# One sum of raw weights per pair of gate and up: VectorE addition or accumulating DMA

## The chip, the cores and the metric

The kernel runs on one core of a Trainium2 chip. The core has five engines that this text calls by their names in the profile: PE (TensorE, the matrix multiplier), PEld (its weight loads), DVE (VectorE), ACT (ScalarE), POOL (GpSimd) and SP (SyncE, which here only issues transfers). The metric is device time in microseconds (us); lower is better. All inputs are float32 in HBM, and the result has to match a float32 reference.

## What is computed

Two decoder layers over 512 tokens of width 1024. Each has a SwiGLU block, a mixing block (sliding-window attention beside a short convolution) and a second SwiGLU block; a norm stands before each and at the end.

```python
def swiglu(h, w_gate, w_up, w_down):          # 1024 -> 2816 -> 1024
    return (jax.nn.silu(h @ w_gate) * (h @ w_up)) @ w_down

def reference(x, ...):
    for l in range(2):
        x = x + 0.5 * swiglu(rms_norm(x, ffn1_norm[l]), ffn1_wg[l], ffn1_wu[l], ffn1_wd[l])
        h = rms_norm(x, mix_norm[l])
        z = h @ w_in[l]
        ...
        x = x + jnp.concatenate([attn_out, conv_out], axis=-1) @ w_out[l]
        x = x + 0.5 * swiglu(rms_norm(x, ffn2_norm[l]), ffn2_wg[l], ffn2_wu[l], ffn2_wd[l])
    return rms_norm(x, final_norm)
```

There are four SwiGLU blocks in all; the text numbers them 1 to 4 in their order.

## The kernel before

**Precision.** Every weight group of 128x1024 float32 values is split before it is used: ACT casts it to a rounded high part (`wh`, 1.04 us), and DVE subtracts that from the raw values to get the low part (`wl`, 1.22 us). Both are in `split`, line 228. PE then makes three products per tile: high by high, high by low, low by high. So each group costs one ACT cast and one DVE subtraction, and PE reads `wl` for the first time in the third matmul on the group (`stream`, line 831 on).

**Seven products instead of eight.** Gate and up are taken together as a matrix of two by two blocks: rows are the two halves of the 1024 inputs, columns are gate and up. Call the blocks a11 and a12 (gate, first and second half of the inputs) and a21 and a22 (up). One such stage of 512 gate and 512 up columns is a *pair* below; a block has `("w", b)` with b = 1, 3, 5, 7, 9. The pair is made with seven products of half the tokens instead of eight, and these take seven forms of the weights, in the order of `FORMS`: a11, a12, s2, s3, s1, a22, s4, where

- s1 = a21 + a22,
- s2 = a11 + s1,
- s3 = a11 + a21,
- s4 = a12 + s2.

Each form is held in two groups, h = 0 and 1, so a pair has 14 groups. PE works on one group for 2.72 us and on one form for 5.44 us. The down-projection of 8 blocks of 128 rows is done likewise, in stages `("s", 1)` and `("s", 5)`; the output projection of the mixing block too. The fourth SwiGLU block has `("s", 1)` and then an end of its own.

**Where the sums are made.** `seven` (line 375) lists the loads of a stage: ten units, a11, s1, a12, s3, a22, each for h = 0 and 1. A unit with two sources is loaded from its first source by SP and then the second source is added to it by an accumulating DMA from POOL (`need_raw`, lines 221 to 223). That is so for s1 (a21, then a22 added) and s3 (a21, then a11 read from HBM a second time and added). The other two sums are made in SBUF while the forms are split, in `need_split`: s2 by a DVE addition into a11 (line 269), and s4 by adding a11, which by then holds s2, into a12. In a pair of gate and up that last one is a DVE addition (line 291); in a stage whose `how` is "share", which is every stage of the down-projection and of the output projection, it is an accumulating DMA from SBUF to SBUF, issued by POOL (line 289).

**What sets the order.** `take_split` is called when PE's work on a group is written out; it asks for the split of the group two further on (`SPLIT_AHEAD` = 2), and for raw loads four or more units ahead of that. There are three buffers for `wh` and three for `wl`, so the split of group n+2 can begin when PE has finished group n-1. There are eight buffers for raw units, so a load waits until the last reader of the unit that held its buffer is done. The instructions are not put in order by hand here: a planner orders each engine's instructions when the kernel is built, by data dependences, by the order of the program text and by its own estimate of durations; `issue_after` puts an instruction behind another. On the chip every engine then works through its list in that fixed order. The loads go through SP's list and the accumulating DMAs through POOL's.

**The first pair of a block.** In the pair b = 1 the first group (a11, h = 0) is split with "far": the low part comes from an accumulating DMA, not from DVE. Around this pair DVE also evicts the first small down-projection (line 1268) and makes and splits the forms of the activations (lines 601 to 606 and 228). In the first block this is arranged differently (`near`).

Of the kernel before, what the change touches and what calls it, by code (L numbers as in the profile page):

```python
# [75 lines left out]
def trunk_kernel(  # L76
# [23 lines left out]
    nc = tc.nc  # L100
# [92 lines left out]
    units = []  # L193
# [6 lines left out]
    def add_unit(*unit):  # L200
        units.append(unit)
        return len(units) - 1
# [24 lines left out]
    def split(hi, lo, raw, eng=nc.vector):  # L227
        return nc.scalar.copy(hi, raw), eng.tensor_sub(lo, raw, f32(hi))  # L228

    def split_far(hi, lo, raw):  # L230

        nc.scalar.activation(lo, raw, AF.Copy, scale=-1.0)
        nc.scalar.copy(hi, raw)
        return nc.gpsimd.dma_start(out=f32(lo), in_=raw, accum_op=ALU.add)

    def need_split(g):
        while state["split"] <= min(g, len(order) - 1):
            n = state["split"]
            u, what = order[n]
            far = what == "far"  # L240
            if what in (None, "far"):
                need_raw(u if far else max(u, min(u + LOAD_AHEAD, state["hold"] or len(units))))
                raw = raw_of.pop(u)
            elif isinstance(what, tuple) and what[0] == "end":

                _, what, h = what
                at = {"a11": 2, "s2": 2, "s3": 3, "s1": 3, "a12": 4, "a22": 5, "s4": 5}[what]
                need_raw(u + 3 * at + h + LOAD_AHEAD)
                raws = {name: u + 3 * i + h for i, name in enumerate(END_LOADS)}
                if what == "s2":  # L250
                    with tc.issue_after(state["rest"]):
                        nc.vector.tensor_add(raw_of[raws["a11"]], raw_of[raws["a11"]], raw_of[raws["s1"]])
                raw = raw_of[raws["a11" if what in ("s2", "s4") else what]]
            elif isinstance(what, tuple):

                what, h, how = what
                far = how == "far"
                last = {"a11": 0, "a12": 4, "s2": 2, "s3": 6, "s1": 2, "a22": 8, "s4": 4}[what]
                need_raw(u + h if far else u + max(last, 4) + h + LOAD_AHEAD)
                a11, s1, a12, s3, a22 = (raw_of.get(u + 2 * i + h) for i in range(5))  # L260
                if what == "s2":

                    late = state["late"] if h else None
                    if not state["late"] and how == "share":
                        late = state["rest"]
                    if how == "behind":
                        late = state["mark"]
                    with tc.issue_after(late) if late else nullcontext():
                        nc.vector.tensor_add(a11, a11, s1)  # L269
                raw = {"a11": a11, "a12": a12, "s2": a11, "s3": s3, "s1": s1, "a22": a22, "s4": a12}[what]  # L270
            shape = list(raw.shape)
            hi = wpool.tile(shape, F32R, tag="wh", bufs=3, name=f"wh_{n}")
            lo = wpool.tile(shape, F32R, tag="wl", bufs=3, name=f"wl_{n}")
            if far:
                sent = split_far(hi, lo, raw)
            else:
                state["cast"], state["rest"] = (i.ins for i in split(hi, lo, raw))
                if isinstance(order[n][1], tuple) and order[n][1][2] == "mark":
                    state["mark"] = state["rest"]
            if isinstance(order[n][1], tuple) and order[n][1][0] == "end":  # L280
                if what == "a12":
                    nc.gpsimd.dma_start(out=raw_of[raws["a11"]], in_=raw, accum_op=ALU.add)
                if what in ("s3", "s1", "a12", "a22"):
                    del raw_of[raws[what]]
                if what == "s4":
                    del raw_of[raws["a11"]]
            elif isinstance(order[n][1], tuple):
                if what == "s3" and how == "share":
                    nc.gpsimd.dma_start(out=a12, in_=a11, accum_op=ALU.add)
                elif what == "s3":  # L290
                    nc.vector.tensor_add(a12, a12, a11)
                done = {"s3": (0, 3), "s1": (1,), "a22": (4,), "s4": (2,)}.get(what, ())
                for i in done:
                    del raw_of[u + 2 * i + h]
            split_of[n] = (hi, lo)
            state["split"] += 1
            if far:

                with tc.issue_after(sent.ins):
                    need_raw(u + LOAD_AHEAD + (4 + h if isinstance(order[n][1], tuple) else 0))  # L300
# [26 lines left out]
    def abreast(kc):  # L327

        return max(1, KC // kc) if kc in (2, 4) else 1
# [34 lines left out]
    def plan():  # L364
        def cols(src, k0, kc, n, how=None, last=False):
            wide = abreast(kc)
            for b in halves_of(n, wide, last):
                order.append((add_unit((src, k0, kc, b * P, wide * P)), how))

        def plain(wg, wu, b):  # L370
            for w in (wg, wu):
                for j in range(2):
                    order.append((add_unit((w, 0, KC, (2 * b + j) * P, P)), None))

        def seven(at, how):


            u = len(units)
            for what in (((0, 0),), ((1, 0), (1, 1)), ((0, 1),), ((1, 0), (0, 0)), ((1, 1),)):
                for h in range(2):  # L380
                    add_unit(*(at(o, j, h) for o, j in what))
            order.extend((u, (what, h, how(what, h))) for what in FORMS for h in range(2))

        def ffn(wg, wu, wd, stages, near=False):
            for what, b in stages:
                how = "far" if b == (0,) and not near else None
                if what == "p":
                    plain(wg, wu, b)
                if what == "w":
                    seven(  # L390
                        lambda o, j, h: ((wg, wu)[o], KC // 2 * j + 2 * h, 2, 2 * b * P, S),
                        lambda what, h: "far"
                        if (b, what, h) == (1, "a11", 0)
                        else {("a12", 0): "mark", ("s2", 1): "behind"}.get((what, h))
                        if near and b == 3
                        else None,
                    )
                if what == "s":
                    seven(
                        lambda o, j, h: (wd, 2 * b + KC // 2 * j + 2 * h, 2, o * S, S),  # L400
                        lambda what, h: "share",
                    )
                if what == "d":
                    cols(wd, 2 * b[0], 2 * len(b), KC, how, len(b) == 2)
                    if len(b) == 2:
                        closing.append(len(units) - 1)
                if what == "e":
                    u = len(units)
                    roomy.update(range(u, u + 3))
                    for form_ in END_LOADS:  # L410
                        ojs = {"s1": ((1, 0), (1, 1)), "s3": ((1, 0), (0, 0))}
                        for i in range(3):
                            add_unit(
                                *(
                                    (wd, 2 * b + (KC + 2 * j if i == 2 else KC // 2 * j + 2 * i), 2, o * S, S)
                                    for o, j in ojs.get(form_, ((0, int(form_ == "a12")) if form_ != "a22" else (1, 1),))
                                )
                            )
                    order.extend((u, ("end", what, i)) for what in END_FORMS for i in range(3))

        for l in range(DEPTH):
            ffn(ffn1_wg[l], ffn1_wu[l], ffn1_wd[l], INNER, l == 0)
            for c in MIX_COLS:
                for j in range(2):
                    order.append((add_unit((w_in[l], 0, KC, (2 * c + j) * P, P)), None))
            seven(
                lambda o, j, h: (w_out[l], KC // 2 * j + 2 * h, 2, o * S, S),
                lambda what, h: "share",
            )
            ffn(ffn2_wg[l], ffn2_wu[l], ffn2_wd[l], INNER if l + 1 < DEPTH else LAST)  # L430
# [1349 lines left out]
```

## Time and profile before

| what | us |
|---|---|
| median of three runs | 1625.92 (1625.47 to 1626.92) |
| profiled execution, its own time | 1628.27 |
| span of its trace, first to last instruction | 1626.5 |
| PE busy | 1616.2 |
| DVE busy | 1367.3 |
| ACT busy | 1177.8 |
| POOL busy | 223.5 |

The span is 1.8 us shorter than the execution's own time: that much lies before its first and after its last instruction. The mean granted clock of PE is 0.999. In rows of the profile, `L228` is line 228 of the kernel; "out<-in" names the tiles with buffer numbers left out, so `wl<-raw,wh` is the making of a low part. In a timeline row the first number is the start, the second the length from the first start to the last end of the merged instructions, `x2` their number, and square brackets hold the engine's idle time ahead of it and what ended it. Instructions that follow one another on DVE overlap by less than 0.1 us, so two rows of 1.22 us take about 2.3 us together.

### The profile page before, as it was taken

How to read it: one execution, taken by the hardware profiler on the slowest of the kernel's cores; microseconds unless marked ns; L12 is line 12 of the kernel's file. 1: busy time of each engine (PE TensorE's matmuls, PEld its weight loads, DVE VectorE, ACT ScalarE, POOL GpSimd, SP SyncE). 2: the span in 40 equal slices, each digit the busy share in tenths (PEclk: the TensorE clock that was granted, in tenths of full speed). 3: DMA queues.
4: the chain of work that ended last, by engine and by line, in shares of the span. 5: the costliest groups of instructions: out<-in, count | busy, mean ns of one | idle time of the engine just before them, and what ended most of it. 6: DMA issues, size and time to landing. Idle time of an engine off the chain costs nothing.

```text
span 1626.5 us, 21177 instructions
## 1 busy us (share of the span) xinstructions
PE 1616.2 (99%) x7571; PEld 1349.5 (83%) x7571; DVE 1367.3 (84%) x1780; ACT 1177.8 (72%) x1511; POOL 223.5 (14%) x199
## 2 busy tenths in 40 slices
PE   9999999999999999999999999999999999999998
PEld 7888888888898878888888888888888988888887
DVE  7978797988899877797999777989788998677997
ACT  6677777857766577778865777788586767878665
POOL 1211111001211111111011111110012111111121
PEclk9999999999999999999999999999999999999999
DMA  9999999912597798999867899999136978999992
GB/s 269 213 231 213 215 215 236 242 58 77 145 230 170 177 218 214 214 218 246 224 147 186 215 216 221 211 245 224 48 91 154 235 149 215 228 221 226 231 264 71
DMA packets 307182, 318.12 MB, mean 196 GB/s; under 512 B 125628, under 2 KB 188676, under 8 KB 307076
## 3 DMA queue, kind: packets, MB, share of 16 engines
q1 hardware_dynamic: 265412, 230.90, 49.6%
q0 software_dynamic: 41200, 85.47, 30.7%
q8 instruction: 59, 0.97, 0.2%
q14 instruction: 47, 0.39, 0.1%
q10 hardware_dynamic: 464, 0.40, 0.1%
HBM read 264.29 MB, written 2.10 MB: 164 GB/s over the span
## 4 chain that ended last, share of the span: by engine, by line
PE 96%; DMA 2%; DVE 1%; ACT 0%; issue 0%; SPq 0%; POOL 0%; DVEq 0%; POOLq 0%
PE x L837 26%; PE y L837 13%; PE x_s L837 9%; PE acc L318 7%; PE acc L319 7%; PE acc L321 7%; PE w L837 7%; PE y_s L837 4%; PE x_m L822 3%; PE w_s L837 3%; PE y_m L822 1%; DMA raw<-in_ffn_wu_dram 1%; PE y_e L837 1%; PE x_e L837 1%; PE acc L699 1%; PE w_m L822 1%
## 5 line engine op out<-in xcount | busy, mean ns | idle before, releaser
L228 DVE TENSOR_TENSOR wl<-raw,wh 128x1024 fp32r<-128x1024 f32 (+1 forms) x494 | 598.7, 1219 | 171.4 <-ACT wh L228 170.3
L228 ACT CAST wh<-raw 128x1024 fp32r<-128x1024 f32 (+1 forms) x494 | 513.8, 1043 | 304.7 <-PE x L837 92.9
L318 PE MATMUL acc<-xh,wh 128*128 128x512 f32 x392 | 153.3, 393 | 0.5 <-ACT wh L228 0.5
L319 PE MATMUL acc<-xl,wh 128*128 128x512 f32 x392 | 153.1, 391 | 0.0
L321 PE MATMUL acc<-xh,wl 128*128 128x512 f32 x384 | 149.6, 390 | 0.0
L223 POOL DMA_DIRECT2D raw<-in_ffn_wu_dram x40 | 50.3, 1268 | 384.3 <-DMA raw<-in_ffn_wu_dram 182.6
L318 PEld LDWEIGHTS acc<-xh,wh 128*128 128x128 f32 x392 | 73.8, 188 | 15.1 <-ACT wh L228 0.6
L319 PEld LDWEIGHTS acc<-xl,wh 128*128 128x128 f32 x392 | 73.7, 188 | 14.4
L321 PEld LDWEIGHTS acc<-xh,wl 128*128 128x128 f32 x384 | 72.1, 188 | 15.2
L223 POOL DMA_DIRECT2D raw<-in_ffn_wg_dram x40 | 49.4, 1248 | 201.8 <-DMA raw<-in_ffn_wu_dram 92.0
L223 POOL DMA_DIRECT2D raw<-in_ffn_wd_dram x34 | 41.1, 1216 | 248.8 <-DMA raw<-in_ffn_wd_dram 86.8
L269 DVE TENSOR_TENSOR raw<-raw,raw 128x1024 f32<-128x1024 f32 x58 | 70.5, 1219 | 5.5 <-issue 3.1
L837 PE MATMUL w<-wl,fb21h 128*128 128x512 f32 x160 | 62.4, 390 | 1.5 <-DVE wl L228 1.5
L1101 ACT COPY raw_a<-turned 128x1024 uint16<-128x1024 uint16 x48 | 63.4, 1355 | 0.0
L837 PE MATMUL x<-wl,fb11h 128*128 128x512 f32 x160 | 62.4, 390 | 0.0
L837 PE MATMUL x<-wl,ft1h 128*128 128x512 f32 x160 | 62.4, 390 | 0.0
L837 PE MATMUL w<-wh,fb21h 128*128 128x512 f32 x160 | 62.3, 390 | 0.0
L837 PE MATMUL y<-wh,ft3h 128*128 128x512 f32 x160 | 62.3, 390 | 0.0
L837 PE MATMUL x<-wh,fb11l 128*128 128x512 f32 x160 | 62.3, 389 | 0.0
L837 PE MATMUL x<-wh,ft2l 128*128 128x512 f32 x160 | 62.3, 389 | 0.0
L837 PE MATMUL x<-wh,ft1h 128*128 128x512 f32 x160 | 62.3, 389 | 0.0
L837 PE MATMUL x<-wh,ft1l 128*128 128x512 f32 x160 | 62.3, 389 | 0.0
(517 smaller groups left out, 4542.3 us busy)
## 6 DMA issues: line engine op xcount, KB each, us to landing
raw<-in_ffn_wu_dram SPq DMA_DIRECT2D x127, 512.0 KB, 5.6
raw<-in_ffn_wd_dram SPq DMA_DIRECT2D x105, 512.0 KB, 6.2
raw<-in_ffn_wg_dram SPq DMA_DIRECT2D x86, 512.0 KB, 5.3
raw<-in_ffn_wu_dram POOLq DMA_DIRECT2D x40, 512.0 KB, 9.2
raw<-in_ffn_wg_dram POOLq DMA_DIRECT2D x40, 512.0 KB, 6.3
raw<-in_w_in_dram SPq DMA_DIRECT2D x36, 512.0 KB, 4.0
raw<-in_ffn_wd_dram POOLq DMA_DIRECT2D x34, 512.0 KB, 9.3
raw<-raw POOLq DMA_DIRECT2D x21, 512.0 KB, 7.4
```

What stands on the lines that cost most here:

```text
L223: nc.gpsimd.dma_start(out=r, in_=rows_of(*more), accum_op=ALU.add)
L228: return nc.scalar.copy(hi, raw), eng.tensor_sub(lo, raw, f32(hi))
L269: nc.vector.tensor_add(a11, a11, s1)
L318: nc.tensor.matmul(acc, hi[:, k, :], rhs[k][0], start=k == first, stop=False)
L319: nc.tensor.matmul(acc, hi[:, k, :], rhs[k][1], start=False, stop=False)
L321: nc.tensor.matmul(acc, lo[:, k, :], rhs[k][0], start=False, stop=k == last)
L699: nc.tensor.matmul(opening[n], (lo if part == "w" else hi)[:, k, :], xl if part == "x" else xh, start=n not in begun, stop=k == KC - 1 and ...
L822: nc.tensor.matmul(accs[c // 2][:, c % 2, :], w[:, k, cols], x_[:, 2 * h + k, :], start=start and c % 2 == 0 and h + k + i == 0, stop=h + ...
L837: nc.tensor.matmul(accs[u], x_[:, 2 * h + k, tok], w[:, k, :], start=start and h + k + i == 0, stop=h + k == 2 and i == 2, skip_group_chec ...
L1101: nc.scalar.copy(words(raws[self.b][:, c, :]), self.to[:, :, c, :])
```

## The change

`seven` gets an argument `here`. With it, unit s3 is only a21, loaded by SP; no accumulating DMA adds a11. Instead, right behind the split of the a12 group of the same h, DVE adds the raw a11 into it.

```diff
             elif isinstance(order[n][1], tuple):
+                if what == "a12" and len(units[u + 6 + h]) == 1:
+                    nc.vector.tensor_add(s3, s3, a11)
                 if what == "s3" and how == "share":
                     nc.gpsimd.dma_start(out=a12, in_=a11, accum_op=ALU.add)
                 elif what == "s3":
                     nc.vector.tensor_add(a12, a12, a11)
...
-        def seven(at, how):
+        def seven(at, how, here=False):
             u = len(units)
-            for what in (((0, 0),), ((1, 0), (1, 1)), ((0, 1),), ((1, 0), (0, 0)), ((1, 1),)):
+            s3 = ((1, 0),) if here else ((1, 0), (0, 0))
+            for what in (((0, 0),), ((1, 0), (1, 1)), ((0, 1),), s3, ((1, 1),)):
...
                         if near and b == 3
                         else None,
+                        here=b < 9 and (b > 1 or not near),
                     )
                 if what == "s":
                     seven(
                         lambda o, j, h: (wd, 2 * b + KC // 2 * j + 2 * h, 2, o * S, S),
-                        lambda what, h: "share",
+                        lambda what, h: None if (b, what) == (1, "s3") else "share",
                     )
```

`here` holds for the pairs b = 1, 3, 5, 7 of the four blocks except b = 1 of the first block (`near`): 15 pairs, 30 accumulating DMAs from HBM. The last part of the diff turns the SBUF-to-SBUF accumulation of s4 in stage `("s", 1)` into the DVE addition of line 291, twice in each of four blocks: 8 DMAs. The sum s3 must come before s2 in the same h, since s2 overwrites a11.

## The prediction

> **What bounds the kernel now.** I read the page first, then the chain of waits in order of time, and then DVE's timeline in three kinds of stages.
>
> ```profile
> span 1626.5 us, 21177 instructions
> ...
> PE 1616.2 (99%) x7571; PEld 1349.5 (83%) x7571; DVE 1367.3 (84%) x1780; ACT 1177.8 (72%) x1511; POOL 223.5 (14%) x199
> ...
> PE 96%; DMA 2%; DVE 1%; ACT 0%; issue 0%; SPq 0%; POOL 0%; DVEq 0%; POOLq 0%
> ...
> L269 DVE TENSOR_TENSOR raw<-raw,raw 128x1024 f32<-128x1024 f32 x58 | 70.5, 1219 | 5.5 <-issue 3.1
> ...
> raw<-in_ffn_wg_dram POOLq DMA_DIRECT2D x40, 512.0 KB, 6.3
> ...
> raw<-raw POOLq DMA_DIRECT2D x21, 512.0 KB, 7.4
> ```
>
> PE is the bound: 96% of the chain is PE. No weight transfer counts unless it makes PE wait, so the question is only where PE waits now and where DVE, which gets the new work, is so late that PE would wait. In the whole trace there is one stall of PE inside the blocks, in the second block's pair b = 3:
>
> ```profile
> 560.11 1.22 DVE L228 TENSOR_TENSOR wl<-raw,wh 128x1024 fp32r<-128x1024 f32 x1
> 564.42 1.22 DVE L269 TENSOR_TENSOR raw<-raw,raw 128x1024 f32<-128x1024 f32 x1 [3.09 <-issue]
> 565.56 1.22 DVE L228 TENSOR_TENSOR wl<-raw,wh 128x1024 fp32r<-128x1024 f32 x1
> 566.70 0.68 DVE L1029 TENSOR_TENSOR p<-p,gate 128x512 f32<-128x512 f32 x1
> 568.39 1.23 DVE L269 TENSOR_TENSOR raw<-raw,raw 128x1024 f32<-128x1024 f32 x1 [1.01 <-DMA raw<-in_ffn_wu_dram]
> 569.53 0.68 DVE L1029 TENSOR_TENSOR p<-p,gate 128x512 f32<-128x512 f32 x1
> 570.13 1.22 DVE L228 TENSOR_TENSOR wl<-raw,wh 128x1024 fp32r<-128x1024 f32 x1
> ```
> ```profile
> 569.48 0.39 PE L837 MATMUL w<-wh,fb21l 128*128 128x512 f32 x1
> 571.41 0.50 PE L837 MATMUL w<-wl,fb21h 128*128 128x512 f32 x1 [1.54 <-DVE wl L228]
> ```
>
> Two s2 additions wait on DVE for accumulating DMAs into s1; the splits behind them wait too, and PE starts a matmul 1.93 us after the one before it, where 0.23 us is usual: 1.7 us lost, some 2.0 with two short slips ahead of it. That is all that faster transfers could give back.
>
> **What is removed.** 30 accumulating DMAs of s3 (512 KB, 6.3 us each) and 8 of the 21 from SBUF to SBUF (7.4 us). They cost PE nothing directly. Their worth is at most the 2.0 us above. But that stall hangs on the accumulations into s1, which stay, so I take 0. The other bound in this pair is a loss: the s3 loads come no earlier than those accumulations.
>
> ```profile
> raw<-in_ffn_wu_dram SPq DMA_DIRECT2D x1, 512.0 KB, 10.4
> ```
>
> This is the second s3 load, issued at 557.7, landed at 568.1. If the planner puts both s3 sums ahead of the s2 additions, DVE starts at 568.1 on six operations of 1.14 us and two of 0.6 (back to back) ahead of 570.13 + 1.22 = 571.35; they end at 576.1, 4.8 us later. So this pair: -2.0 to +4.8, taken at 0, since DVE also idles 3.09 + 1.01 us there, enough for both sums.
>
> **What is added.** 38 additions on DVE of the shape of L269: 1.219 us alone, 1.14 back to back. 38 x 1.14 = 43 us on an engine busy for 84%. Whether they cost depends on the slack of the stage.
>
> *Down-projection, b = 1 (8 additions).* They fall behind the s3 split. In the second block:
>
> ```profile
> 735.35 1.22 DVE L228 TENSOR_TENSOR wl<-raw,wh 128x1024 fp32r<-128x1024 f32 x1 [1.04 <-ACT wh L228]
> 738.66 1.23 DVE L228 TENSOR_TENSOR wl<-raw,wh 128x1024 fp32r<-128x1024 f32 x1 [2.09 <-ACT wh L228]
> 743.01 1.23 DVE L228 TENSOR_TENSOR wl<-raw,wh 128x1024 fp32r<-128x1024 f32 x1 [3.12 <-ACT wh L228]
> ```
>
> Idle time of 2.09 + 3.12 us covers 2 x 1.14. Cost 0; without that cover 2.3 us in each of four stages. The a12 buffer is whole sooner, so nothing is late behind it.
>
> *Pairs b = 3, 5, 7 (24 additions, 12 pairs).* The third block's b = 5 stands for them; two load rows come first (s3, h = 0 issued at 917.5; h = 1 at 920.3), then DVE.
>
> ```profile
> raw<-in_ffn_wu_dram SPq DMA_DIRECT2D x1, 512.0 KB, 8.6
> ```
> ```profile
> raw<-in_ffn_wu_dram SPq DMA_DIRECT2D x1, 512.0 KB, 7.1
> ```
> ```profile
> 922.68 1.22 DVE L228 TENSOR_TENSOR wl<-raw,wh 128x1024 fp32r<-128x1024 f32 x1
> 923.93 1.23 DVE L269 TENSOR_TENSOR raw<-raw,raw 128x1024 f32<-128x1024 f32 x1
> 925.08 1.22 DVE L228 TENSOR_TENSOR wl<-raw,wh 128x1024 fp32r<-128x1024 f32 x1
> ...
> 928.80 1.23 DVE L228 TENSOR_TENSOR wl<-raw,wh 128x1024 fp32r<-128x1024 f32 x1 [0.17 <-ACT wh L228]
> ...
> 933.60 1.22 DVE L228 TENSOR_TENSOR wl<-raw,wh 128x1024 fp32r<-128x1024 f32 x1
> 935.83 0.69 DVE L1014 TENSOR_TENSOR gate<-w,p 128x512 f32<-128x512 f32 x1 [1.02 <-PE w L837]
> ```
> ```profile
> 932.00 0.39 PE L837 MATMUL w<-wl,fb21h 128*128 128x512 f32 x1
> ```
>
> The loads have landed at 926.1 and 927.4. In the program text the sums stand behind the third and fourth split (928.80 and the next), when both loads are there. They then push the fifth split from 934.8 to at most 937.1. PE needs it two groups (5.44 us) after the matmul at 932.00, at 937.4. That fits, with 0.3 us left, and the 1.02 us of idle at 935.8 takes up part of the rest. Cost taken 0 in 11 pairs (the twelfth is the one with the stall). The other bound is below as a rival: up to 2.3 us a pair.
>
> *Pairs b = 1 of blocks 2, 3 and 4 (6 additions).* Here DVE has no gap. Over the stretch that ends with the fifth split, in each block:
>
> ```profile
> 513.00:536.00 23.00, 23.00 (x103) 19.04 (x102) 22.62 (x26) 13.19 (x15) 3.88 (x4) 1.00 0.77 157
> 838.00:860.00 22.00, 22.00 (x99) 18.14 (x98) 21.66 (x25) 12.33 (x14) 3.40 (x4) 1.00 0.80 166
> 1318.00:1341.00 23.00, 23.00 (x107) 19.11 (x106) 22.63 (x26) 14.34 (x19) 3.34 (x3) 1.00 0.79 161
> ```
>
> The columns are stretch, length, then PE, PEld, DVE, ACT and POOL busy: DVE is at work for 98%. In each block, the fifth and sixth splits (s2) on DVE, and PE's first read of the fifth one's low part:
>
> ```profile
> 531.67 2.35 DVE L269 TENSOR_TENSOR raw<-raw,raw 128x1024 f32<-128x1024 f32 x2
> 533.95 1.21 DVE L228 TENSOR_TENSOR ft1l<-hf,ft1h 128x1024 fp32r<-128x1024 f32 x1
> 535.08 2.35 DVE L228 TENSOR_TENSOR wl<-raw,wh 128x1024 fp32r<-128x1024 f32 x2
> ...
> 859.49 2.35 DVE L228 TENSOR_TENSOR wl<-raw,wh 128x1024 fp32r<-128x1024 f32 x2
> ...
> 1340.55 2.35 DVE L228 TENSOR_TENSOR wl<-raw,wh 128x1024 fp32r<-128x1024 f32 x2
> ```
> ```profile
> 536.76 0.39 PE L837 MATMUL x<-wl,ft2h 128*128 128x512 f32 x1
> ...
> 861.28 0.39 PE L837 MATMUL x<-wl,ft2h 128*128 128x512 f32 x1
> ...
> 1342.01 0.39 PE L837 MATMUL x<-wl,ft2h 128*128 128x512 f32 x1
> ```
>
> The fifth split ends 1.22 us after its start: at 536.30, 860.71 and 1341.77. Slack is 0.46, 0.57 and 0.24 us. Both s3 sums must run before it: one of them because s2 overwrites a11, the other by the program text. Two additions cost 533.95 - 531.67 = 2.28 us. The stalls: 2.28 - 0.46 = 1.82, 2.28 - 0.57 = 1.71, 2.28 - 0.24 = 2.04; together 5.6 us. The other bound: work that is not needed by then (the second s2 addition, a sum or split for the activations) falls behind the fifth split, two steps of 1.14 us, and the cost is 0. I take 5.6, since in all three blocks DVE did those steps ahead of the fifth split.
>
> **The sum.** 0 (transfers) + 0 (down-projection) + 0 (12 pairs) + 5.6 = +5.6 us on the profiled 1628.27, thus 1633.9. The median of the runs shown is 2.35 us under the profiled execution; on it the sum is 1625.92 + 5.6 = 1631.5.
>
> **Rivals.** (A) *Sums that wait for loads.* The planner brings additions forward: L269 ran at 923.93, between the first and second split, though the text has it behind the fourth. If it brings the s3 sum there too, DVE waits until 926.16 for the load. Then come s3 sum, s2 addition, second split, s3 sum, s2 addition (1.14 each), two operations of 0.6 and the third split (1.22), which ends at 934.3 instead of 930.0; PE needs it at 932.0. That is 2.3 us a pair, in 11 pairs 25 us; with half the additions in front some 1.1 us, 12 us in all. For it: the stall at 564.42 shows the mechanism. Against it: the plan can put the sums behind the third split. Time 1625.9 + 5.6 + 12 = 1643.5, up to 1657. The Trainium skill says in "TensorE: Matmul & The Clock Gate", Specifications, that the queues of VectorE are strict first-in, first-out; the trace agrees, in that the split at 565.56 stood behind the waiting addition, and by a queue that could be passed this rival would cost 0 instead of 12 to 25 us.
>
> (B) *Not slower: the gap-free stretch is rearranged, and the transfers give back the stall.* In pair b = 1 the planner puts the two deferrable steps behind the fifth split, so the 5.6 us are gone; with 15.7 MB (30 x 512 KB) less to move, the s1 accumulations land earlier and some or all of the 2.0 us stall goes. For it: the stall waits for a DMA. Against it: DVE's 98%, and in that stretch no s3 accumulation is in flight beside s1's. Time 1625.9 - 2.0 = 1623.9 to 1625.9; it decides if fewer than 2 x 1.14 us of the added work stand ahead of the fifth split.
>
> (C) *The change does not do what it says*, because a planner's new order removes other stalls or adds them elsewhere: no stall of over 0.5 us is there to remove apart from the one shown. Chance 0.02.
>
> **Chances and range.** Forecast 0.40, from 1629.2 to 1634; A 0.21; B 0.37; C 0.02. "Within 0.2%" (3.3 us) is about what a measurement of this kernel can tell from no change. All of the forecast and A is slower by more, and part of C: 0.62. B lies within it but for a tail: 0.35 same, 0.03 faster, as a gain of 3.3 us exceeds the stall. The range leaves out the upper half of A and the end of B: 1624.0 to 1645.0. The forecast's own range is 1629 to 1636.
>
> **What would show it.** Right: in the changed trace PE waits 1.7 to 2.0 us for `wl` at the fifth group of the pair b = 1 of blocks 2, 3 and 4, with DVE at 98% before it; DVE busy is 43 us more; the pairs b = 3, 5, 7 keep 38.1 us; the accumulations of gate weights fall from 40 to 10 and those from SBUF to SBUF from 21 to 13. Wrong: pairs b = 3, 5, 7 longer, with DVE waiting for `raw<-in_ffn_wu_dram` at the new line (A); or no stall in b = 1 and none at 569 (B).

## The result and the profile after

| what | before | after |
|---|---|---|
| median, us | 1626.04 (1625.47 to 1626.92) | 1669.99 (1665.57 to 1674.16) |
| profiled execution, its own time | 1628.27 | 1674.16 |
| span of its trace | 1626.5 | 1672.4 |
| mean granted clock of PE | 0.999 | 0.992 |

The ratio is 1.0264, with an interval of 1.0248 to 1.0281: slower by 44 us. The forecast was 1631.5, so its direction was right and its size was not; the time also lies above the stated range.

The page of the changed kernel, in the lines that answer to those shown of before:

```profile
span 1672.4 us, 21118 instructions
...
PE 1633.6 (98%) x7571; PEld 1355.0 (81%) x7571; DVE 1405.9 (84%) x1818; ACT 1176.6 (70%) x1511; POOL 180.0 (11%) x161
...
HBM read 248.56 MB, written 2.10 MB: 150 GB/s over the span
...
PE 81%; DVE 7%; issue 5%; DMA 4%; ACT 2%; SPq 0%; POOL 0%; DVEq 0%; ACTq 0%; POOLq 0%
...
L289 DVE TENSOR_TENSOR raw<-raw,raw 128x1024 f32<-128x1024 f32 x30 | 36.7, 1222 | 55.5 <-issue 35.7
...
raw<-raw POOLq DMA_DIRECT2D x13, 512.0 KB, 6.1
```

Line 289 is the new sum. DVE is busy for 38.6 us more (1405.9 - 1367.3), where the forecast had 43 for the 38 additions. But the chain of waits, which was 96% PE, now has 16% of DVE, DMA and "issue", and ahead of the new sum DVE stood idle for 55.5 us. The view of that one line says until what it was idle (us, times):

```profile
  issue: 35.7, 7
  DMA raw<-in_ffn_wu_dram: 19.7, 6
```

These are 13 waits, from 1.6 to 6.9 us: the sum of h = 0 in each of the twelve pairs b = 3, 5 and 7, and one in a pair b = 1. No sum of h = 1 waited. What PE waited for (us in total, times, longest):

```profile
PE x L841 <- DVE wl L228: 24.9, 10, 4.6
```

**One pair, step by step.** This is block 2, the start of the pair b = 7, on DVE:

```profile
648.86 1.23 DVE L228 TENSOR_TENSOR wl<-raw,wh 128x1024 fp32r<-128x1024 f32 x1 [1.49 <-ACT wh L228]
650.00 0.68 DVE L1029 TENSOR_TENSOR u<-y,u 128x512 f32<-128x512 f32 x1
656.93 1.22 DVE L289 TENSOR_TENSOR raw<-raw,raw 128x1024 f32<-128x1024 f32 x1 [6.25 <-issue]
658.08 0.68 DVE L1030 TENSOR_TENSOR u<-u,gate 128x512 f32<-128x512 f32 x1
658.68 0.68 DVE L1029 TENSOR_TENSOR u<-y,u 128x512 f32<-128x512 f32 x1
659.28 1.22 DVE L228 TENSOR_TENSOR wl<-raw,wh 128x1024 fp32r<-128x1024 f32 x1
```

The row at 659.28 is the first split of this pair. The sum for the *fourth* form of the pair stands ahead of it, and even ahead of three of the four evictions of the pair before (lines 1029 and 1030). The sum needs the s3 load. SP's two issues of such loads, and then the time from issue to landing of the first, stand in the trace so:

```profile
647.40 3.08 SPq L210 DMA_DIRECT2D raw<-in_ffn_wu_dram  x2
```
```profile
raw<-in_ffn_wu_dram SPq DMA_DIRECT2D x1, 512.0 KB, 9.5
```

647.40 + 9.45 = 656.85, and the sum starts at 656.93. So the idle time that the profile puts down to "issue" is the wait for this load. At the same time PE does this:

```profile
655.96 0.39 PE L841 MATMUL x<-wh,fb11h 128*128 128x512 f32 x1
656.19 0.39 PE L841 MATMUL x<-wh,fb11l 128*128 128x512 f32 x1
660.55 0.50 PE L841 MATMUL x<-wl,fb11h 128*128 128x512 f32 x1 [3.97 <-DVE wl L228]
...
661.35 0.63 PE L841 MATMUL x<-wl,fb11h 128*128 128x512 f32 x1
661.78 0.63 PE L841 MATMUL x<-wh,fb11h 128*128 128x512 f32 x1
...
664.76 0.40 PE L841 MATMUL x<-wh,fb11l 128*128 128x512 f32 x1
664.99 0.40 PE L841 MATMUL x<-wl,fb11h 128*128 128x512 f32 x1
```

It stalls at its first read of `wl`, for 4.36 us from start to start where 0.23 is usual. And then, from 661.35 to 664.76, a matmul starts every 0.427 us instead of every 0.227: eight steps, 1.6 us lost once more.

**The whole account.** For each pair I summed the start-to-start distances of PE's matmuls above 0.227 us, and took the runs of 0.427 us as "half speed":

| us lost by PE | before | after | forecast (change) |
|---|---|---|---|
| pairs b = 1, blocks 2 to 4 | 0.2 | 5.0 | 5.6 |
| pairs b = 3 | 2.1 | 5.2 | 0 |
| pairs b = 5 | 0 | 15.9 | 0 |
| pairs b = 7 | 0 | 10.4 | 0 |
| down-projections | 0 | 0 | 0 |
| half speed | 0 | 10.6 | no term |

The sums are 47 and 2 us, and the spans differ by 45.9, so nothing else is needed to explain the time. On DVE the waiting sum stands between the first and the second split in the four pairs b = 3 and in b = 7 of the first block, and ahead of the first split, as shown above, in the other seven. Those five lose 1.3 us each (5.2 + 1.4; in b = 7 of the first block at the fifth group), those seven 3.6 (15.9 + 10.4 - 1.4 = 24.9), and nearly all of the half speed follows the seven.

### The profile page after: what moved, and what is told of

The parts are those of the page before. It is cut to its first block, busy times and chain, and to the rows that moved or that the text cites. A ratio compares the mean times of both kernels' runs of the same rounds, so it can differ in the third digit from the quotient of the medians.

```text
span 1672.4 us, 21118 instructions
## 1 busy us (share of the span) xinstructions
PE 1633.6 (98%) x7571; PEld 1355.0 (81%) x7571; DVE 1405.9 (84%) x1818; ACT 1176.6 (70%) x1511; POOL 180.0 (11%) x161
## 4 chain that ended last, share of the span: by engine, by line
PE 81%; DVE 7%; issue 5%; DMA 4%; ACT 2%; SPq 0%; POOL 0%; DVEq 0%; ACTq 0%; POOLq 0%
PE x L841 21%; PE y L841 10%; PE x_s L841 9%; PE acc L320 6%; PE acc L321 6%; PE acc L323 6%; PE w L841 5%; PE y_s L841 5%; DMA raw<-in_ffn_wu_dram 3%; DVE wl L228 3%; PE x_m L826 3%; PE w_s L841 3%; PE y_m L826 1%; ACT wh L228 1%; PE y_e L841 1%
## 5 line engine op out<-in xcount | busy, mean ns | idle before, releaser
L841 PE MATMUL x<-wl,fb11h 128*128 128x512 f32 x160 | 68.1, 426 | 24.3 <-DVE wl L228 23.8
L289 DVE TENSOR_TENSOR raw<-raw,raw 128x1024 f32<-128x1024 f32 x30 | 36.7, 1222 | 55.5 <-issue 35.7
L269 DVE TENSOR_TENSOR raw<-raw,raw 128x1024 f32<-128x1024 f32 x58 | 70.4, 1219 | 0.6 <-DMA raw<-in_ffn_wu_dram 0.5
L841 PE MATMUL x<-wh,fb11h 128*128 128x512 f32 x160 | 66.9, 418 | 0.0
L841 PE MATMUL x<-wh,fb11l 128*128 128x512 f32 x160 | 66.4, 415 | 0.0
L841 PE MATMUL y<-wh,ft4h 128*128 128x512 f32 x160 | 62.5, 390 | 1.0 <-ACT wh L228 1.0
L841 PE MATMUL x<-wl,ft2h 128*128 128x512 f32 x160 | 61.9, 390 | 1.1 <-DVE wl L228 1.1
L841 PE MATMUL y<-wh,ft3l 128*128 128x512 f32 x160 | 62.3, 390 | 0.0
```

The lines of the kernel that those rows point to most:

```text
L289: nc.vector.tensor_add(s3, s3, a11)
L841: nc.tensor.matmul(accs[u], x_[:, 2 * h + k, tok], w[:, k, :], start=start and h + k + i == 0, stop=h + k == 2 and i == 2, skip_group_chec ...
```

## The experiments

The theory after the result: the sum *waits for its load* in front of a split, and all else follows. The rivals: the added *work* is too much for DVE; or the traffic itself slows PE.

**1. The sum behind the splits** (`e1_behind`). `state["rest"]` is the low part of the split just made, so the sum cannot pass the split of a12.

```diff
-                    nc.vector.tensor_add(s3, s3, a11)
+                    with tc.issue_after(state["rest"]):
+                        nc.vector.tensor_add(s3, s3, a11)
```

> All of the change, but each s3 sum is put behind the split of its a12 group on DVE, where the loads have landed. Theory W (the loss is DVE standing still in front of s3 sums that wait for a load, with PE behind it): the waits of 3 to 7 us in pairs b = 3, 5, 7 are gone and with them 35 to 40 us; what stays is the first pair of blocks 2 to 4, so 1626 to 1633. Rival D (the loss is 43 us more work on DVE): the work is the same, so 1655 to 1672.

Measured: 1636.19 us, ratio 1.0042 (1.0025 to 1.0059). The same 30 sums (line 290 here) waited for nothing, and no matmul ran at half speed. 9.0 us of stalls were left: 3.7 in the pairs b = 1, seven of about 0.7 in pairs b = 5 and 7, and shorter slips. DVE in block 3, b = 5 shows why:

```profile
933.02 1.23 DVE L228 TENSOR_TENSOR wl<-raw,wh 128x1024 fp32r<-128x1024 f32 x1 [0.24 <-PE x L842]
934.16 1.22 DVE L290 TENSOR_TENSOR raw<-raw,raw 128x1024 f32<-128x1024 f32 x1
935.30 1.22 DVE L228 TENSOR_TENSOR wl<-raw,wh 128x1024 fp32r<-128x1024 f32 x1
936.43 1.22 DVE L290 TENSOR_TENSOR raw<-raw,raw 128x1024 f32<-128x1024 f32 x1
937.57 2.36 DVE L269 TENSOR_TENSOR raw<-raw,raw 128x1024 f32<-128x1024 f32 x2
939.84 1.22 DVE L294 TENSOR_TENSOR raw<-raw,raw 128x1024 f32<-128x1024 f32 x1
940.98 2.36 DVE L228 TENSOR_TENSOR wl<-raw,wh 128x1024 fp32r<-128x1024 f32 x2
```

Ahead of the fifth split (940.98) stands line 294, the s4 addition, which is not needed until the seventh form.

**2. That addition behind its split too** (`e6_both_behind`).

```diff
-                    nc.vector.tensor_add(a12, a12, a11)
+                    with tc.issue_after(state["rest"]):
+                        nc.vector.tensor_add(a12, a12, a11)
```

> As e1_behind, and each s4 addition is put behind the split of its s3 group too, so that it no longer stands ahead of the fifth split. In e1_behind eight of the pairs b = 5, 7 stalled 0.69 us at the fifth split (5.5 us in all) and the pairs b = 1 3.7 us. Theory W with DVE's order as the rest: the 5.5 us go, about 1631. If the two added sums are too much work for the stretch whatever their order: no change, 1636.

Measured: 1631.83 us, 1.0032 (1.002 to 1.0044). The stalls of 0.7 us are gone; 3.6 us are left in the pairs b = 1 (2.13, 0.85, 0.64). One stall is new: in block 4's own end, at 1573.91, PE starts 1.7 us late, behind a DVE eviction (line 1340). The median is 5.3 us above that of before in the same round (1626.54), and 3.6 + 1.7 = 5.3. So 44 us became some 5 us by order alone, with every transfer and every addition of the change still there.

**3. The pairs b = 1 left out of it** (`e7_no_first`): number 2 with `here=1 < b < 9`.

> As e6_both_behind, without the s3 sum on DVE in the pairs b = 1 (12 pairs, 24 sums, and the 8 of the down-projection stay). Theory W: nothing waits and all work is covered, 1625 to 1627.5, no worse than before. Rival D: 32 more operations on DVE cost some us still, 1630 or more.

Measured: 1628.28 us, 1.0007 (0.9998 to 1.0017), with 0.6 us of stalls in the pairs and the down-projections. 24 of the 30 sums and all eight additions in the down-projection are in it, and 12.6 MB (24 x 512 KB) of accumulations are not: no gain, and by the interval no loss that can be told from none. But the trace has the new stall of number 2 again (1.7 us, at 1570.59), and the median lies 1.7 us above 1626.54.

**4. The pairs b = 1 alone** (`e3_first_pair`): the changed kernel with `here=b == 1 and not near` and the down-projection as before.

> The s3 sum on DVE in the pair b = 1 of blocks 2, 3 and 4 alone (6 sums); all other sums as before. The prediction's step: +5.6 us, 1631.6. The trace of the changed kernel shows stalls of 1.98, 2.52 and 0.52 us there, together 5.0: 1631. If the stalls only moved there from later pairs: 1626 to 1628.

Measured: 1631.35 us, 1.0021 (1.0011 to 1.003), about 3.4 us. The stalls in these pairs are 1.98, 1.11 and 0.52 us, 3.6 together. The traced execution took 1635.56 us, with 3.1 us of further stalls in block 2's down-projection; the other nine took 1630.78 to 1631.85.

**5. The down-projection alone** (`e4_down`): the changed kernel with `here=False`.

> Only the down-projection's part: 8 additions on DVE instead of SBUF-to-SBUF accumulations in stage b = 1. Theory W and the prediction: covered by idle time, 1625.5 to 1627. Rival: 8 x 1.14 us uncovered, up to 1635.

Measured: 1626.77 us, 0.9989 (0.998 to 0.9998). Eight additions in place of DMAs cost nothing.

**6. More work without the change's transfers** (`e2_work`): the kernel before, with one more DVE operation per group (the maximum of a12 with itself) in the pairs b = 3, 5 and 7.

```diff
+                if what == "a11" and u in marked:
+                    nc.vector.tensor_tensor(out=a12, in0=a12, in1=a12, op=ALU.max)
```

> The kernel before, with its accumulating DMAs, plus two more DVE operations of the size of a sum (the maximum of a12 with itself, which leaves it as it is) in each of the 12 pairs b = 3, 5, 7, free to be placed as early as a12 has landed, which is some 5 us ahead of s3. Theory W: 24 x 1.14 us of work without a wait for s3 costs 0 to 4 us, 1626 to 1630. Rival D: 24 of 38 operations, so some 28 us, about 1654.

Measured: 1645.32 us, 1.0095 (1.007 to 1.012). It was meant to show work without a wait, and it didn't: the new operations were put early, and waited themselves, for the a12 load. Their group of DVE:

```profile
L290 DVE TENSOR_TENSOR raw<-raw 128x1024 f32<-128x1024 f32 x24 | 29.4, 1225 | 32.9 <-DMA raw<-in_ffn_wg_dram 32.8
```

So this run does not separate the two. It shows the same mechanism with another load: 32.9 us of idle DVE ahead of 24 operations, and 15.5 us of stalls of PE.

**7. The wait without the work** (`e10_wait_alone`).

```diff
-                    nc.vector.tensor_add(s3, s3, a11)
+                    nc.vector.tensor_add(s3[:, 0:1, 0:P], s3[:, 0:1, 0:P], a11[:, 0:1, 0:P])
```

> The changed kernel with the sum s3 made in 128 of its 1024 columns only (the rest of the sum is left out, so this kernel computes something else): the wait for the s3 load stays where it is, a tenth of the work remains. Theory 'the wait': the stalls in b = 3, 5, 7 stay but for the 1.1 us of work in each, 15 to 25 us with some 4 to 10 us of half speed, and those of b = 1 go: 1644 to 1664 us. Rival 'the work': without the work the time is that of before within some us, 1626 to 1631 us.

Measured: 1669.19 us, 1.0269 (1.0251 to 1.0288), as slow as the full change. The place shown above, in this kernel:

```profile
648.18 0.68 DVE L1029 TENSOR_TENSOR u<-y,u 128x512 f32<-128x512 f32 x1
653.59 0.29 DVE L289 TENSOR_TENSOR raw<-raw,raw 128x128 f32<-128x128 f32 x1 [4.72 <-issue]
653.80 0.68 DVE L1030 TENSOR_TENSOR u<-u,gate 128x512 f32<-128x512 f32 x1
```

The operation takes 0.29 instead of 1.22 us, and DVE waits ahead of it as before. The time came out above the expected 1644 to 1664, because the shorter operation was put in front in more places: its 18 waits sum to 62.0 us (40.3 and 21.7), among them one of 5.26 us in a pair b = 1. The rival "work" had 1626 to 1631 and falls.

**8. Why the load is late** (`e11_no_s1_transfers`): the changed kernel without the accumulations into s1 in the same 15 pairs.

```diff
+            s1 = s3 if here else ((1, 0), (1, 1))
-            for what in (((0, 0),), ((1, 0), (1, 1)), ((0, 1),), s3, ((1, 1),)):
+            for what in (((0, 0),), s1, ((0, 1),), s3, ((1, 1),)):
```

> The changed kernel without the accumulating DMAs into s1 in the 15 pairs that the change touches (s1 is a21 alone, so this kernel computes something else); every load and every VectorE operation stays. Theory 'the load is slowed': the s3 load takes 8 to 9.5 us instead of some 5 because it moves beside two accumulations into s1; without them it lands 3 to 4 us earlier, the waits ahead of the s3 sum fall from 3 to 7 us to 0 to 3, and the time is 1630 to 1645 us. Rival 'the load is issued late', since its buffer comes free late: the landing comes as late as in the changed kernel, within 1 us, and the time stays at 1660 to 1672 us.

Measured: 1630.91 us, 1.0027 (1.0017 to 1.0037). Again the same pair. The sum has the same place in DVE's order; the second row is the load that it waits for, issued at 633.52:

```profile
636.13 0.68 DVE L1030 TENSOR_TENSOR u<-y,u 128x512 f32<-128x512 f32 x1
637.29 1.23 DVE L289 TENSOR_TENSOR raw<-raw,raw 128x1024 f32<-128x1024 f32 x1 [0.47 <-DVE u L1030]
638.43 0.69 DVE L1031 TENSOR_TENSOR u<-u,gate 128x512 f32<-128x512 f32 x1
639.03 0.68 DVE L1030 TENSOR_TENSOR u<-y,u 128x512 f32<-128x512 f32 x1
639.63 1.22 DVE L228 TENSOR_TENSOR wl<-raw,wh 128x1024 fp32r<-128x1024 f32 x1
```
```profile
raw<-in_ffn_wu_dram SPq DMA_DIRECT2D x1, 512.0 KB, 3.7
```

The load takes 3.7 us instead of 9.5; the idle time ahead of all 30 sums falls from 55.5 to 5.9 us, and the pairs b = 3, 5 and 7 lose 0.4 us together. A sum in this place costs nothing if its load arrives. In the changed kernel two accumulations into s1 are under way at that point; the rows of their issue, just ahead of the s3 load's:

```profile
raw<-in_ffn_wu_dram POOLq DMA_DIRECT2D x2, 512.0 KB, 10.6
raw<-in_ffn_wg_dram SPq DMA_DIRECT2D x1, 512.0 KB, 8.3
```

The load in the last row, of a12, takes 8.3 us here and 3.7 in number 8 (issued there at 630.80), so both loads are slower beside the accumulations. What the accumulations take without the loads was not measured. So the loss has two conditions: the early place, and the s1 accumulations beside the load.

**9. The s3 load ahead of the a12 load** (`e9_load_first`), with the sum still free to move:

```diff
+            mid = (s3, ((0, 1),)) if here else (((0, 1),), s3)
-            for what in (((0, 0),), ((1, 0), (1, 1)), ((0, 1),), s3, ((1, 1),)):
+            for what in (((0, 0),), ((1, 0), (1, 1)), *mid, ((1, 1),)):
```

> All of the change, nothing put behind anything, but s3 is loaded ahead of a12 in the pairs that sum on DVE, two loads (about 5.4 us) sooner. Theory W: the wait ahead of each h = 0 sum, 3 to 7 us, falls by some 5 us, so the loss of 44 us falls to 5 to 20 us: 1631 to 1646. Rival D, same work in about the same places: 1665 to 1674.

Measured: 1659.9 us, 1.0216 (1.0189 to 1.0244): a miss. With the load the sums moved forward as well (line 291 here, block 2, b = 5):

```profile
602.67 1.23 DVE L291 TENSOR_TENSOR raw<-raw,raw 128x1024 f32<-128x1024 f32 x1 [0.58 <-DVE p L1031]
603.82 0.68 DVE L1031 TENSOR_TENSOR p<-p,x 128x512 f32<-128x512 f32 x1
604.41 1.22 DVE L229 TENSOR_TENSOR wl<-raw,wh 128x1024 fp32r<-128x1024 f32 x1
608.75 1.23 DVE L291 TENSOR_TENSOR raw<-raw,raw 128x1024 f32<-128x1024 f32 x1 [3.12 <-issue]
609.90 1.22 DVE L229 TENSOR_TENSOR wl<-raw,wh 128x1024 fp32r<-128x1024 f32 x1
```

The sum of h = 0 hardly waits here, and that of h = 1 does, ahead of the last split of the pair before (609.90; PE waited 0.5 us for it); the pair's own first split comes behind that, at 613.43, and PE waited for it again. In all, DVE idles 44.2 us ahead of this line. An earlier load alone took off 10 of the 44 us, no more, because the planner put the sum earlier with it.

**10. DVE held without any wait** (`e5_dose`): the kernel before, with chains of 3 to 12 operations ahead of the first split of eight pairs.

```diff
+            if isinstance(order[n][1], tuple) and order[n][1][:2] == ("a11", 0):
+                with tc.issue_after(state["rest"]):
+                    for _ in range(probes.get(u, 0)):
+                        nc.vector.tensor_tensor(out=raw, in0=raw, in1=raw, op=ALU.max)
```

> The kernel before, with chains of 3 to 12 additional VectorE operations (maximum of a11 with itself, 1.14 us each back to back) ahead of the first split of eight pairs b = 3 and b = 7; they wait for no transfer. Theory 'VectorE held': what matters is that VectorE is occupied in front of the first split, by work or by a wait alike. A chain of d operations then costs 1.14 x d less a slack of 2 to 3 us: d = 3 about 0.5 to 2 us, d = 6 about 4 us, d = 12 about 11 us, and after stalls of over some 2.5 us PE issues its matmuls every 427 ns instead of 227 for 3 to 5 us, so that 0.8 to 2.6 us come on top. 55 operations in all: 55 x 1.14 - 8 x 2.7 = 41 us of stalls and 8 to 14 us of half speed, about 1627 + 50 = 1677 us. Rival 'the transfers': matmuls at half speed come from the transfers that were waited for; then the stalls of these chains show no row of 427 ns behind them, and the time is about 1668 us.

Measured: one run, 1698.18 us. The first stall of PE in each pair, over 0.227 us:

| operations | 3 | 4 | 5 | 6 | 7 | 8 | 10 | 12 |
|---|---|---|---|---|---|---|---|---|
| stall, us | 1.12 | 3.31 | 4.59 | 5.85 | 7.11 | 8.37 | 10.89 | 13.41 |

From 4 on this is 1.26 us for each operation less 1.7: once the slack is used up, PE loses what DVE is held, one for one. The time is higher than expected since a dependent operation takes 1.26 us and not 1.14, the slack is 1.7 us and not 2.7, and some 1.2 us of shorter slips follow each of the longer stalls. The last of the eight, on PE and in the view by stretches (stretch, length, then busy time of PE, PEld, DVE, ACT, POOL, PE's granted clock, DMA share and GB/s):

```profile
1499.41 0.39 PE L845 MATMUL x<-wl,fb22h 128*128 128x512 f32 x1
1513.05 0.79 PE L845 MATMUL x<-wh,fb11h 128*128 128x512 f32 x1 [13.25 <-ACT wh L230]
...
1515.75 0.63 PE L845 MATMUL x<-wl,fb11h 128*128 128x512 f32 x1
1516.18 0.63 PE L845 MATMUL x<-wh,fb11h 128*128 128x512 f32 x1
```
```profile
1513.00:1518.00 5.00, 4.91 (x11) 3.45 (x12) 4.98 (x5) 4.29 (x4) 0.00 (x0) 0.51 0.00 0
1518.00:1523.00 5.00, 5.00 (x24) 4.08 (x23) 4.36 (x5) 3.47 (x5) 0.00 (x0) 1.00 0.00 0
```

The half speed is there although nothing waited for a transfer, and DMA was idle. It comes from PE's own idle time.

**11. The old stall in block 2, b = 3** (`e8_second_behind`): the kernel before with number 5's down-projection, and the kernel's own "mark" and "behind" order for the pair b = 3 of every block.

```diff
-                        if near and b == 3
+                        if b == 3
```

> The kernel before with the down-projection's part of the change, and in every pair b = 3 the second s2 addition put behind the third split, as block 1 already has it. No s3 sum is on DVE. If the 2.0 us stall of block 2 comes from the split standing behind a waiting addition, it goes: 1624. If it comes from the accumulations themselves being late: 1626, no change.

Measured: 1626.47 us, 0.9997 (0.9988 to 1.0007). In the trace the stall of 2.05 us is gone and the span is 1624.4, 2.1 us shorter. The medians do not show it; 2 us are 0.12%, within the interval. It may be that most executions do not have this stall: the traced execution of before took 1628.27 us and that of number 5, whose trace has the stall too, 1628.29, 2.2 and 1.5 us above the medians of the others; here the traced one took 1626.17. Only one trace of each kernel was kept, so this is not shown. No version measured here is faster than before.

## Why the prediction was partly right

- **What bounds the kernel, and transfers removed at 0:** right. Number 3 has 24 of the 30 accumulations removed and gained nothing. The removal of the accumulations was never worth more than the one stall of 2 us.
- **Down-projection at 0:** right (number 5, and no stall in the trace of after).
- **Pairs b = 1 at 5.6 us:** DVE's part was right, PE's part was not, and the size was too large. As forecast, both sums and all other steps stand ahead of the fifth split: in block 2 of the changed kernel it ends at 548.59 (547.37 + 1.22), 1.7 us after the third matmul of its group was due (546.46 + 2 x 0.227 = 546.91). But PE did not wait for this `wl`, as the forecast's sign had it. What the working left out is that PE's order is planned anew as well: the two stalls of block 2 are waits for ACT's `wh` of later forms, 1.06 us at this place and 0.67 at the sixth form. The three pairs lose 5.0 us in the changed kernel. In number 2, where no sum waits, the term measures 3.6 us (2.13, 0.85 and 0.64 against the forecast's 1.82, 1.71 and 2.04); 3.6 us again in number 4. Block 4 in the changed kernel:

```profile
1374.88 0.39 PE L841 MATMUL x<-wh,ft2l 128*128 128x512 f32 x1
1375.33 0.50 PE L841 MATMUL y<-wh,ft3h 128*128 128x512 f32 x1
1375.67 0.39 PE L841 MATMUL x<-wl,ft2h 128*128 128x512 f32 x1
```

  The products of the late `wl` were moved behind high-part products, here those of `ft3h`, so PE reads it later than the third matmul, and less is lost.
- **Pairs b = 3, 5, 7 at 0 in 11 pairs: this step failed.** It took the sums where the program text has them, behind the third and fourth split, "when both loads are there". In the changed kernel the sum of h = 0 stands behind the first split in five pairs and ahead of it in seven. Numbers 2 and 3 show that the assumed order, with the s4 additions behind their splits too, would indeed have cost nothing in these pairs; numbers 1, 7 and 8 show that the place and the load decide.
- **Rival A was the one that happened**, with its mechanism, its line and its sign named. It put the sum between the first and the second split, at up to 2.3 us a pair; where the sum did go there, it cost 1.3. What it did not see is the place ahead of the first split: there a wait of 4.3 to 6.9 us falls on work that PE needs next, at 3.6 us a pair. Its upper end was 25 us; the stalls of these twelve pairs came to 31.5. And the half speed that followed them, 10.6 us, was in no term.
- **The load took no longer than the working had it.** In the pair that stood for all, the first s3 load took 8.6 us. In the eleven of the twelve pairs where the trace has its landing, it took 7.1 to 10.0 us before and 7.5 to 10.1 us after, each time beside the two s1 accumulations. What forecast and rival had wrong is where the sum stands on DVE when the load lands.
- **The chances:** the forecast's case with its b = 1 term got 0.40 and A 0.21. The clue for A was in the rows quoted (L269 run at 923.93, two splits ahead of its place in the text), and it should have had the greater weight: what was moved forward once, with an operand just arrived, can be moved again.

What stays open: why the plan put these sums so early. Its estimate of when a load lands is not in any trace; that it differs from the chip's 9.5 us is an inference from the order. It was not tried to change that estimate.

## What to carry to other kernels

An operation that waits on a strictly ordered engine costs the wait, not its own length: with a quarter of the length the loss was the same, and behind the urgent work it was nothing. When a DMA is replaced by an engine's operation, ask which transfer that operation waits for, beside what traffic that transfer lands, and what stands behind it in the queue; where an order is planned by a program, pin the operation behind the work that the bound engine needs next. And price a stall of two microseconds or more on PE with the half-speed stretch after it.

## What the hardware showed that was not expected

**Half speed after short stalls.** After a stall PE can run at a granted clock of 0.50 for a while. The view by stretches has, for the stall shown step by step above (4.13 us):

```profile
657.92:661.33 3.41, 0.78 (x3) 0.67 (x4) 3.41 (x6) 0.66 (x1) 0.00 (x0) 1.00 0.00 0
661.33:664.74 3.41, 3.41 (x9) 2.65 (x8) 3.41 (x5) 0.59 (x1) 0.00 (x0) 0.50 0.00 0
664.74:668.15 3.41, 3.41 (x16) 2.82 (x15) 3.41 (x4) 1.91 (x3) 0.00 (x0) 1.00 0.00 0
```

PE starts 9 matmuls in the middle stretch and 16 in the last, which is as long. Mostly seven to nine starts are affected and some 1.6 us lost, whether the stall lasted 4.6 or 13.4 us; after that of 4.78 us it was thirteen starts and 2.6 us. In the changed kernel and in numbers 7 and 10, all nine stalls of over 4 us were followed by half speed; of eleven from 1.96 to 3.31 us six were, and five were not (a stall of 2.18 us was, one of 2.92 was not).

So the length of a stall alone does not decide. The granted clock in these traces changes only at points of a grid with steps of 3.413 us: in the changed kernel half speed begins, after its stalls, at 128.85, 661.33, 954.88, 995.84, 1446.39 and 1490.77, which lie 156, 86, 12, 132 and 13 steps apart, and lasts one step, or two after the stall of 4.78 us. Between 20 and 1600 us of all thirteen traces, every step at full clock in which PE lost 0.61 or more of the time (in starts more than 0.227 us apart) was followed by one at half clock (19 steps), and none in which it lost 0.59 or less. The stall of 2.18 us lay within one step and took 0.64 of it; that of 2.92 us fell into two, with 0.49 of the first lost and 0.40 of the second.

The Trainium skill describes this in "TensorE: Matmul & The Clock Gate", Part 1: the array's clock is at half rate after an idle window of about 3.4 us and back at full rate after a busy one, and the window runs free of the kernel. The length of the steps and their fixed grid agree. That a window has to be idle as a whole does not: 0.61 of one was enough, and with it stalls of 1.96 to 2.37 us in four cases.

**Loads beside accumulations.** A load of 512 KB took 9.5 us with two accumulating DMAs under way, and 3.7 us in the same place without them (number 8).
